# Two input projections moved between the quarters of a state-space output, and a silu rewritten by tanh

## The chip, the cores and the metric

The kernel runs on one core of one Trainium2 chip. The metric is device time in microseconds of one launch, lower is better. The core has TensorE (PE, the matmuls), VectorE (DVE), ScalarE (ACT), GpSimd (POOL) and SyncE (SP, which issues the weight DMAs). All engines read one static order of instructions each, and meet by semaphores.

## What is computed

Two layers of a decoder trunk on 272 tokens (16 meta tokens and 256), width 1024, all in float32. Each layer is a half-step feed-forward block, a mixer and another half-step feed-forward block. The change lies in the mixer alone:

```
proj = rmsnorm(h) @ w_in        # columns: sb q, k, v | deltanet qkv, z, b, a | s5 u
o_sb = rmsnorm(stick_breaking_attention(q, k, v))
o_dn = rmsnorm(gated_delta_rule(silu(conv(qkv)), b, a), dn_out_norm) * silu(z)
y    = gelu(s5_scan(u));  o_s5 = rmsnorm(y * sigmoid(y @ w_glu + b_glu))
h   += concat(o_sb, o_dn, o_s5) @ w_out
```

So z is wanted only by the last product of the DeltaNet group, and v only by the attention's outputs.

## The kernel before

Activations lie transposed, 128 channels by 272 tokens. Every product with a weight matrix is made of three matmuls in a 32-bit matmul type with a high and a low part (`mm3`, lines 144 to 146): high by high, high by low, low by high. `weights` (L134 to L139) loads 512 KB of weights, casts the high part on ACT (L136) and makes the low part by a subtraction on DVE, or on POOL for the calls of a mixer whose running number stands in `ON_POOL` (5, 7, 10, 15, 20, 25). The raw tile has 3 buffers, the high part 3, the low part 2. One **unit** is one such load and the 24 matmuls of one block of 128 output channels; `proj` (L1364) then scales it on DVE out of PSUM.

PSUM tiles go by tags (`a` to `d`) of two buffers each, and a tag's buffers are given out in the order of the program text. So a tile of a tag waits for the tile two before it in the text, whatever its priority. Here the `b` tag is used in this order: the increments of the S5 scan (`pinc`, L821, four quarters of two tiles), then the DeltaNet's `pn`, `pl`, `plt`, `pv`, `pvt` (L1088 to L1111), then the four quarters of S5's outputs (`pY`, L850 and L852). The `c` tag is used by the transposes of v (`pvs`, L1216) and after them by the attention's scores (`pz`, L1227 to L1231); `pvn`, `pS`, `pk`, `pkt` and the DeltaNet's inverse (`px` and `py`, L1016 to L1068, by `dn_inverse`) use `d`.

A scheduler orders the instructions of each engine ahead of time by its own estimate of when they are ready; `high_priority` blocks go first among those that are ready: `first()` (4000) for the DeltaNet, `second()` (1500) for S5's outputs, the GLU and its root; the rest goes by the order of the text. The steps of a mixer are written in the order of `ORD = "czsrqgbmn"`: four more convolution units, the z units with their silu, the S5 scan, the DeltaNet's rest, the six units of q, k and v, S5's outputs with the GLU, the attention, the root of S5, the DeltaNet's norm. After them `WOUT = "SnY"` gives the output projection: the S5 rows, the last products of the DeltaNet (`dn_out`), the other rows.

`s5_outputs` makes, for each of four quarters, 12 float32 matmuls into one `b` tile and four gelu activations out of it. `glu` then splits the result (L1278, L1279), multiplies it by two weight tiles (`pglu`) and takes a tanh (L107).

Of the kernel before, what the change touches and what calls it, by code (L numbers as in the profile page):

```python
# [13 lines left out]
AF = mybir.ActivationFunctionType  # L14
ALU = mybir.AluOpType
# [3 lines left out]
P = 128  # L19
NMETA = 16  # L20
SEQ = 256
T = NMETA + SEQ
# [6 lines left out]
DEPTH = 2  # L29
NQ = 16  # L30
NCH = T // 4
# [6 lines left out]

FIRST, SECOND, URGENT, THIRD = 4000, 1500, 0, 0
SBP = 0  # L40
ORD = "czsrqgbmn"
WOUT = "SnY"
OTAG, NTAG, ZT = "d", "c", "cccd"
HORD = (0, 1, 4, 2, 5, 3, 8, 6, 7, 9)
# [6 lines left out]
SET_SILU = "silu_and_others"  # L51
# [4 lines left out]
def bc(ap, axis, n):  # L56
    return ap.unsqueeze(axis).to_broadcast([*ap.shape[:axis], n, *ap.shape[axis:]])


def f32(ap):  # L60
    return ap.bitcast(F32)


class Trunk:
    def __init__(self, ctx, tc, a, out):
        self.ctx, self.tc, self.nc, self.a, self.out = ctx, tc, tc.nc, a, out
        pool = lambda n, b, **k: ctx.enter_context(tc.tile_pool(name=n, bufs=b, **k))
        self.const = pool("const", 1)
        self.res = pool("res", 1)
        self.raw = pool("raw", NBUF[2])  # L70
        self.wsp = pool("wsp", 2)
        self.small = pool("small", 1)
        self.ps = pool("ps", 1, space=PSUM)
        self.load_ins, self.set = None, None
        self.first = []
        self.since = []
        self.nw = 0
        self.on_pool = ()
        self.blocks = (0, 4)


    def psum(self, tag, nm):
# [58 lines left out]

    def mm3(self, p, wh, wl, xh, xl, first, last):
        mm = self.nc.tensor.matmul
        mm(p, wh, xh, start=first, stop=False)  # L144
        mm(p, wh, xl, start=False, stop=False)  # L145
        mm(p, wl, xh, start=False, stop=last)  # L146

# [125 lines left out]
    def load_params(self, prm):  # L273
        nc, a, c = self.nc, self.a, self.const
        q = nc.sync
        row = 0
        at = {}
        for nm, pat in (("ffn1_norm", "l (b p) -> (l b) p"), ("mix_norm", "l (b p) -> (l b) p"),
                        ("ffn2_norm", "l (b p) -> (l b) p"), ("s5_out_norm", "l (b p) -> (l b) p"),
                        ("s5_b_glu", "l (b p) -> (l b) p"), ("dn_conv_w", "l k (b p) -> (l k b) p")):  # L280
            src = a[nm].rearrange(pat, p=P)
            n = src.shape[0]
            q.dma_start(prm[row:row + n, :], src)
            at[nm] = (row, n)
# [12 lines left out]
        self.s5g = g("s5_out_norm", pat="p (l b) -> p l b", l=DEPTH)  # L297
        self.bglu = g("s5_b_glu", pat="p (l b) -> p l b", l=DEPTH)
        self.cw = g("dn_conv_w", pat="p (l k b) -> p l k b", l=DEPTH, k=4)

        for t in (self.s5g, self.bglu):
            nc.vector.tensor_scalar(t, t, 0.5, None, op0=ALU.mult)
        self.dng = g("dn_out_norm", pat="p (l b) -> p l b", l=DEPTH)
        self.sbg = g("sb_out_norm", pat="p (l b) -> p l b", l=DEPTH)

    def finish_params(self, t, sel):
# [532 lines left out]
            V.tensor_tensor(z[:, 1, :, 1:], w[:, 1, :, :-1], x[:, 0, :, :-1], op=ALU.add)  # L839
            self.S.append(z)  # L840

    def s5_outputs(self, u):

        A, PE = self.nc.scalar, self.nc.tensor
        for r in range(4):
            p = self.psum("b", "pY")
            for b in range(4):
                q = 4 * b + r
                po = p[:, b * NCH:(b + 1) * NCH]
                PE.matmul(po, self.M0[:, q, :], self.U[:, r, b, :], start=True, stop=False)  # L850
                for k in range(2):
                    PE.matmul(po, self.W2[k][:, q].rearrange("p k g c -> p (k g c)"), self.S[r][:, k, b], start=False, stop=k == 1)  # L852
            for t in range(4):
                o = u[32 * r:32 * r + 32, :, t * NCH:t * NCH + NCH]
                self.act(o, p[32 * t:32 * t + 32, :T].rearrange("p (b c) -> p b c", b=4), AF.Gelu_apprx_tanh)

# [15 lines left out]
    @staticmethod  # L872
    def hsl(h):
        return slice(64 * (h % 2), 64 * (h % 2) + 64)
# [307 lines left out]
        self.newton(r, R, t)  # L1182
        V.tensor_tensor(o, o, bc(r, 2, 64), op=ALU.mult)

    def dn_out(self, zg, slot):

        nc = self.nc
        V, G, A, PE = nc.vector, nc.gpsimd, nc.scalar, nc.tensor
        o, hsl = self.o, self.hsl
        od = self.dn_tile([P, 2, 64], "od")  # L1190
        G.tensor_copy(od, bc(o[:, 8], 1, 2))
        for b in range(2):
            po = self.psum("d", "po")
            for c in range(2):
                PE.transpose(po[:, c * P:c * P + P], o[:, 4 * c + 2 * b:4 * c + 2 * b + 2].rearrange("p h d -> p (h d)"), self.ident)
            PE.transpose(po[:, 256:256 + P], od.rearrange("p x d -> p (x d)"), self.ident)
            y = self.c288("dy")[:, :T]
            V.tensor_tensor(y[:, :256], po[:, :256], zg[:, b, :256], op=ALU.mult)
            for h in (2 * b, 2 * b + 1):
                V.tensor_tensor(y[hsl(h), 256:T], po[hsl(h), 256 + 32 * h:256 + 32 * h + 16], zg[hsl(h), b, 256:T], op=ALU.mult)  # L1200
            A.activation(self.xh[:, slot + b, :], y, AF.Copy)
            V.tensor_tensor(self.xl[:, slot + b, :], y, f32(self.xh[:, slot + b, :]), op=ALU.subtract)


    def sb(self, l, q, k, v, slot):
# [111 lines left out]
    def mixer(self, l, nxt):  # L1317
        nc, a = self.nc, self.a
        V, G, A, PE = nc.vector, nc.gpsimd, nc.scalar, nc.tensor
        w_in, w_out = a["w_in"][l], a["w_out"][l]  # L1320
        t0 = NMETA if l == DEPTH - 1 else 0
        first = lambda: self.tc.high_priority(FIRST)
        second = lambda: self.tc.high_priority(SECOND)
        self.norm_end()
        R = self.R
        self.on_pool, self.nw = ON_POOL, -1
        with ExitStack() as es:
# [26 lines left out]
            u = tmp.tile([P, 4, T], F32, name="s5u")  # L1354
            for b in range(4):
                p, = self.unit(w_in[:, 1800 + b * P:1800 + b * P + P], P, "ba"[b % 2])
                i = lambda t: t.rearrange("p (c j) -> p c j", j=4)
                V.tensor_tensor(u[:, b, :].rearrange("p (j c) -> p c j", j=4), i(p[:, :T]), i(R), op=ALU.mult)
            zr = tmp.tile([P, 2, T], F32, name="pz")

            def proj(c0, dst):
                for b in range(2):
                    p, = self.unit(w_in[:, c0 + b * P:c0 + b * P + P], P)
                    V.scalar_tensor_tensor(dst[:, b, :], p[:, :T], 0.125 if c0 == 0 else 1.0, R, op0=ALU.mult, op1=ALU.mult)  # L1364

            q, k, v = (tmp.tile([P, 2, T], F32, name=f"p{n}") for n in "qkv")

            def do_z():
                proj(1536, zr)
                self.phase(SET_SILU)  # L1370
                for b in range(2):
                    self.act(zr[:, b, :], zr[:, b, :], AF.Silu)
                    V.tensor_scalar(zr[:, b, :], zr[:, b, :], self.dng[:, l], None, op0=ALU.mult)

            def do_s5():
                with self.tc.high_priority(THIRD):
# [4 lines left out]
                    self.dn_rest(qkv)  # L1381

            def do_qkv():
                for c0, dst in ((0, q), (256, k), (512, v)):
                    proj(c0, dst)

            def do_sb():
                with self.tc.high_priority(SBP):
# [8 lines left out]
            def do_glu():  # L1397
                with second():
                    self.phase(SET_GELU)
                    self.s5_outputs(u)  # L1400
                    self.acc = self.glu(l, u)
                    self.phase(SET_LNEXP)

# [4 lines left out]
            def do_r5():  # L1408
                with second():
                    self.rms(self.acc, 4 * 512, 0, self.R5, "b")  # L1410

            steps = dict(z=do_z, s=do_s5, r=do_rest, q=do_qkv, b=do_sb, c=do_conv, g=do_glu, n=do_norm, m=do_r5)
            for x in ORD:
                steps[x]()

# [23 lines left out]
            for x in WOUT:  # L1439
                if x == "n":  # L1440
                    with first():
                        self.dn_out(zr, 2)
                    continue
                if x == WOUT[-1]:
                    self.norm_begin(*nxt)
                for d0 in (4, 6, 0, 2):
                    w_out_part(x, d0, "ab"[d0 // 2 % 2])
                    if x == WOUT[-1]:
                        for d in {4: (4, 5), 6: (6, 7), 0: (), 2: (0, 1, 2, 3)}[d0]:
                            self.norm_block(d, d0 == 2, t0)  # L1450
# [44 lines left out]
```

## Time and profile before

| | us |
|---|---|
| median of 3 runs | 1191.51 (1189.88 to 1191.59) |
| the profiled execution, its own time | 1194.31 |
| its span, first to last instruction | 1192.5 |
| TensorE busy | 1154.8 (97%) |
| VectorE busy | 853.6 (72%) |
| ScalarE busy | 614.1 (52%) |
| mean granted clock of TensorE | 0.972 |

The page of the profile cuts the span into 40 slices and gives each engine's busy share and the clock that TensorE was granted (1.00 is 2.4 GHz, 0.50 is 1.2 GHz). The two mixers lie at about 230 to 400 and 818 to 995 us, and there alone the slices show a lower clock and idle time of TensorE. Busy time of TensorE is no measure of its speed: a matmul at half the clock is busy twice as long.

### The profile page before, as it was taken

The page shows a single profiled execution, that of the slowest core. Times are in us where ns is not written, and L with a number is a line of the kernel's source. Part 1 is how long each engine was busy: PE and PEld are TensorE (multiplying, and loading weights), DVE is VectorE, ACT ScalarE, POOL GpSimd, SP SyncE. Part 2 cuts the span into 40 slices and gives each one's busy share as a digit, 9 for nine tenths or more (in the row PEclk, how much of TensorE's full clock was granted, in tenths as well). Part 3 has the DMA queues.
Part 4 walks back from the last instruction along what each step waited for, and adds up shares of the span by engine and source line. Part 5 has one row for each costly group of instructions (what it writes and reads, how often), then busy time and mean ns, then how long its engine had stood idle before and what let it go on. Part 6 is the DMA issues. An engine that isn't in the chain of part 4 may idle for free.

```text
span 1192.5 us, 23762 instructions
## 1 busy us (share of the span) xinstructions
PE 1154.8 (97%) x9544; PEld 1104.5 (93%) x9544; DVE 853.6 (72%) x1648; ACT 614.1 (52%) x981; POOL 175.3 (15%) x210
## 2 busy tenths in 40 slices
PE   8999999999998999999999999999999989999997
PEld 7999999998786999999999999999988969999985
DVE  7999986699636866555579998756994268666644
ACT  6455575564166654444455556645632566555533
POOL 6312100021010111110201112011210001111100
PEclk9999999999789999999999999999997599999999
DMA  5656545543201455555565555455431015666663
GB/s 182 179 175 180 166 135 160 167 125 108 71 19 54 142 175 177 168 176 171 177 187 177 169 173 172 132 175 156 124 112 33 27 45 185 181 188 191 187 191 117
DMA packets 196858, 173.74 MB, mean 146 GB/s; under 512 B 21300, under 2 KB 193004, under 8 KB 196748
## 3 DMA queue, kind: packets, MB, share of 16 engines
q1 hardware_dynamic: 196732, 172.22, 48.2%
q8 instruction: 75, 1.23, 0.4%
q14 instruction: 35, 0.29, 0.1%
q10 hardware_dynamic: 16, 0.00, 0.0%
HBM read 171.15 MB, written 1.05 MB: 144 GB/s over the span
## 4 chain that ended last, share of the span: by engine, by line
PE 84%; DVE 10%; ACT 3%; issue 1%; DMA 1%; SPq 0%; ACTq 0%; DVEq 0%
PE proj L146 17%; PE proj L145 17%; PE proj L144 17%; PE pd L146 5%; PE pd L145 5%; PE pd L144 5%; PE pd L493 5%; DVE wl L139 2%; PE pY L852 1%; DVE qkv L1346 1%; DVE xT L1437 1%; PE pY L850 1%; PE pl L887 1%; PE pm L783 1%; PE pz L1227 1%
## 5 line engine op out<-in xcount | busy, mean ns | idle before, releaser
L144 PE MATMUL proj<-xh,wh 128*128 128x272 f32 (+1 forms) x1840 | 521.1, 289 | 6.3 <-DVE sy L1435 2.8
L145 PE MATMUL proj<-xl,wh 128*128 128x272 f32 (+1 forms) x1840 | 518.4, 287 | 0.2 <-DVE xl L1296 0.2
L146 PE MATMUL proj<-xh,wl 128*128 128x272 f32 (+1 forms) x1840 | 492.8, 290 | 3.3 <-DVE wl L139 3.0
L136 ACT ACTIVATE wh<-raw 128x1024 fp32r<-128x1024 f32 (+1 forms) x324 | 338.2, 1044 | 292.8 <-PE proj L145 99.5
L139 DVE TENSOR_TENSOR wl<-raw,wh 128x1024 fp32r<-128x1024 f32 (+1 forms) x312 | 378.4, 1213 | 146.6 <-PE pd L146 60.9
L144 PEld LDWEIGHTS proj<-xh,wh 128*128 128x128 f32 x1840 | 345.4, 188 | 10.5 <-DVE sy L1435 4.1
L145 PEld LDWEIGHTS proj<-xl,wh 128*128 128x128 f32 x1840 | 345.2, 188 | 3.0 <-issue 1.5
L146 PEld LDWEIGHTS proj<-xh,wl 128*128 128x128 f32 x1840 | 328.8, 187 | 7.2 <-DVE wl L139 5.8
L144 PE MATMUL pd<-hh,wh 128*128 128x272 f32 x528 | 149.6, 288 | 0.0
L145 PE MATMUL pd<-hl,wh 128*128 128x272 f32 x528 | 149.3, 288 | 0.0
L435 POOL TENSOR_TENSOR hl<-h,hh 128x272 fp32r<-128x272 f32 (+1 forms) x88 | 81.1, 924 | 452.9 <-ACT hh L434 452.8
L146 PE MATMUL pd<-hh,wl 128*128 128x272 f32 x528 | 140.8, 288 | 0.2
L144 PEld LDWEIGHTS pd<-hh,wh 128*128 128x128 f32 x528 | 99.2, 188 | 0.2
L145 PEld LDWEIGHTS pd<-hl,wh 128*128 128x128 f32 x528 | 99.3, 188 | 0.1
L146 PEld LDWEIGHTS pd<-hh,wl 128*128 128x128 f32 x528 | 95.1, 188 | 1.0 <-DVE wl L139 0.9
L107 ACT ACTIVATE g<-g 128x272 f32<-128x272 f32 (+2 forms) x92 | 37.6, 415 | 68.9 <-DVE g L429 68.8
L433 DVE TENSOR_TENSOR h<-proj,g 128x272 f32<-128x272 f32 (+1 forms) x88 | 37.7, 433 | 32.9 <-PE proj L146 21.3
L434 ACT ACTIVATE hh<-h 128x272 fp32r<-128x272 f32 (+1 forms) x88 | 36.4, 419 | 47.1 <-DVE h L433 47.1
L429 DVE TENSOR_TENSOR g<-proj,R 128x272 f32<-128x272 f32 (+1 forms) x88 | 37.5, 430 | 17.8 <-PE proj L146 17.6
L139 POOL TENSOR_TENSOR wl<-raw,wh 128x1024 fp32r<-128x1024 f32 x12 | 30.7, 2557 | 110.5 <-ACT th L107 34.9
L431 DVE TENSOR_TENSOR g<-g,R 128x272 f32<-128x272 f32 (+1 forms) x88 | 37.7, 432 | 12.6 <-ACT g L107 12.3
L376 POOL TENSOR_TENSOR acc<-acc,sq 128x272 f32<-128x272 f32 (+1 forms) x20 | 22.7, 1134 | 91.4 <-ACT sq L370 90.5
(490 smaller groups left out, 1310.1 us busy)
## 6 DMA issues: line engine op xcount, KB each, us to landing
raw<-in_ffn_w_gate_dram SPq DMA_DIRECT2D x88, 512.0 KB, 3.6
raw<-in_ffn_w_up_dram SPq DMA_DIRECT2D x88, 512.0 KB, 3.6
raw<-in_ffn_w_down_dram SPq DMA_DIRECT2D x70, 512.0 KB, 3.5
raw<-in_w_in_dram SPq DMA_DIRECT2D x36, 512.0 KB, 4.4
raw<-in_ffn_w_down_dram SPq DMA_DIRECT2D x24, 384.0 KB, 3.0
raw<-in_w_out_dram SPq DMA_DIRECT2D x16, 512.0 KB, 3.5
raw<-in_s_w_glu_dram SPq DMA_DIRECT2D x4, 512.0 KB, 3.4
xin<-in_x_dram SPq DMA_DIRECT2D x4, 256.0 KB, 5.8
```

The lines of the kernel that those rows point to most:

```text
L107: i = self.nc.scalar.activation(out, in_, func, **k)
L136: nc.scalar.activation(h[:, :n], r[:, :n], AF.Copy)
L139: e.tensor_tensor(l[:, :n], r[:, :n], f32(h[:, :n]), op=ALU.subtract)
L144: mm(p, wh, xh, start=first, stop=False)
L145: mm(p, wh, xl, start=False, stop=False)
L146: mm(p, wl, xh, start=False, stop=last)
L429: V.tensor_tensor(g1, pg[j][:, :N], R, op=ALU.mult)
L431: V.tensor_tensor(g1, g1, R, op=ALU.mult)
L433: V.tensor_tensor(h, pu[j][:, :N], g1, op=ALU.mult)
L434: nc.scalar.activation(hh[:, f, :N], h, AF.Copy)
L435: G.tensor_tensor(hl[:, f, :N], h, f32(hh[:, f, :N]), op=ALU.subtract)
L493: PE.matmul(pd[i][e], x[:, f, ts], w[:, 0, e * 512:e * 512 + 512], start=f == 0 and w is h and x is hh, stop=f == NF - 1 and w is lo)
```

## The change

The z units leave their place behind the convolutions and the v units theirs behind k. `s5_outputs` now makes one quarter at a time, and after each quarter comes one unit: v's two blocks, then z's two. An ordering edge (no semaphore, both are on TensorE) puts the first matmul of each unit behind the last matmul of its quarter. The units, their weight loads and casts are now written inside the `second()` block, and ahead of the GLU's. Since the running number of the weight calls shifts, the call numbered 10 (on POOL) is q's first block in place of z's first, and number 15 is v's second in place of k's second.

z's silu is no longer one Silu activation and a multiplication by the norm's gain: it is a tanh of z/2 (ACT), then (tanh + 1) z in one DVE operation. The factor one half goes into the gain `dng`, which is halved once at the start; the gain itself is applied in `dn_out` as the scale of the two operations that split the product.

```diff
-ORD = "czsrqgbmn"
+ORD = "csrqgbmn"
     def mm3(self, p, wh, wl, xh, xl, first, last):
-        mm(p, wh, xh, start=first, stop=False)
+        i = mm(p, wh, xh, start=first, stop=False)
+        if self.behind is not None:
+            self.order(getattr(i, "ins", i), self.behind)
+            self.behind = None
-        for t in (self.s5g, self.bglu):
+        for t in (self.s5g, self.bglu, self.dng):
             nc.vector.tensor_scalar(t, t, 0.5, None, op0=ALU.mult)
     def dn_out(self, zg, g, slot):
-            A.activation(self.xh[:, slot + b, :], y, AF.Copy)
-            V.tensor_tensor(self.xl[:, slot + b, :], y, f32(self.xh[:, slot + b, :]), op=ALU.subtract)
+            A.activation(self.xh[:, slot + b, :], y, AF.Copy, scale=g)
+            V.scalar_tensor_tensor(self.xl[:, slot + b, :], y, g, f32(self.xh[:, slot + b, :]), op0=ALU.mult, op1=ALU.subtract)
-            def do_z():
-                proj(1536, zr)
-                self.phase(SET_SILU)
-                for b in range(2):
-                    self.act(zr[:, b, :], zr[:, b, :], AF.Silu)
-                    V.tensor_scalar(zr[:, b, :], zr[:, b, :], self.dng[:, l], None, op0=ALU.mult)
+            def do_z(b):
+                proj(1536, zr, b)
+                t = self.cv("zt")[:, :T]
+                self.act(t, zr[:, b, :], AF.Tanh, scale=0.5)
+                V.scalar_tensor_tensor(zr[:, b, :], t, 1.0, zr[:, b, :], op0=ALU.add, op1=ALU.mult)
             def do_qkv():
-                for c0, dst in ((0, q), (256, k), (512, v)):
+                for c0, dst in ((0, q), (256, k)):
             def do_glu():
                 with second():
                     self.phase(SET_GELU)
-                    self.s5_outputs(u)
+                    units = (proj, 512, v, 0), (proj, 512, v, 1), (do_z, 0), (do_z, 1)
+                    for r, (f, *args) in enumerate(units):
+                        self.behind = self.s5_outputs(u, r)
+                        f(*args)
                     self.acc = self.glu(l, u)
```

`s5_outputs(u, r)` is the body of the old loop over r, and returns its last matmul; `proj(c0, dst, b)` is the body of the old loop over b.

## Rows read from the trace of the kernel before

**Rows 1.** The page: busy us and share of the engines; the granted clock by slice.
```profile
PE 1154.8 (97%) x9544; PEld 1104.5 (93%) x9544; DVE 853.6 (72%) x1648; ACT 614.1 (52%) x981; POOL 175.3 (15%) x210
...
PEclk9999999999789999999999999999997599999999
```
**Rows 2.** Busy us by stretch, first mixer: window, length, PE PEld DVE ACT POOL, clock, DMA.
```profile
264.00:308.00 44.00, 39.89 (x315) 37.42 (x313) 43.68 (x90) 16.82 (x26) 7.86 (x7) 1.00 0.41 120
308.00:325.00 17.00, 16.86 (x292) 13.99 (x292) 9.17 (x20) 1.17 (x5) 0.11 (x1) 0.51 0.10 33
325.00:343.10 18.10, 17.30 (x303) 16.56 (x296) 3.33 (x8) 8.91 (x24) 3.18 (x5) 0.96 0.01 3
343.10:357.80 14.70, 13.74 (x95) 13.10 (x95) 7.60 (x13) 9.46 (x19) 2.61 (x1) 0.82 0.13 37
357.80:384.80 27.00, 23.92 (x175) 17.87 (x175) 16.45 (x43) 17.43 (x37) 0.44 (x1) 1.00 0.19 59
```
**Rows 3.** The same view of three of the four mixer stretches at half the clock.
```profile
341.69:348.52 6.83, 5.99 (x31) 5.80 (x30) 1.92 (x5) 2.88 (x9) 0.74 (x1) 0.50 0.00 0
898.08:911.72 13.64, 13.64 (x294) 10.83 (x297) 6.85 (x16) 1.07 (x3) 0.11 (x1) 0.50 0.02 4
...
925.38:949.27 23.89, 23.46 (x119) 22.29 (x118) 4.88 (x15) 9.71 (x23) 2.35 (x1) 0.50 0.07 23
```
**Rows 4.** VectorE by line, 264 to 309 us: shapes, count, busy us, mean ns.
```profile
L139 DVE TENSOR_TENSOR wl<-raw,wh 128x1024 fp32r<-128x1024 f32 x8 | 9.7, 1211 | 0.0
```
**Rows 5.** Engines in time: start, us, engine, line, operation, shapes, [idle before it <- by].
```profile
276.29 0.42 DVE L1364 SCALAR_TENSOR_TENSOR pz<-proj,R 128x272 f32<-128x272 f32 x1
276.64 1.20 DVE L139 TENSOR_TENSOR wl<-raw,wh 128x1024 fp32r<-128x1024 f32 x1
277.77 0.74 DVE L989 TENSOR_TENSOR r<-LT,id 128x576 f32<-128x576 f32 x1
...
279.56 0.34 DVE L1373 TENSOR_SCALAR pz<-pz,prm 128x272 f32<-128x272 f32 x1
```
**Rows 6.** The same for GpSimd and VectorE, about 287 us.
```profile
286.55 3.10 POOL L139 TENSOR_TENSOR wl<-raw,wh 128x1024 fp32r<-128x1024 f32 x1 [1.42 <-PE proj L146]
...
288.08 1.64 DVE L1006 TENSOR_TENSOR TT<-TT,t 128x54 f32<-128x54 f32 x1
```
**Rows 7.** The same for TensorE, 304 to 309 us and about 325 us.
```profile
307.36 0.54 PE L1216 MATMUL pvs<-ident,pv 128*128 128x128 f32 x2 [2.11 <-DVE pv L1364]
308.14 0.99 PE L1088 MATMUL pn<-bd,sq 128*128 128x2 f32 x4 [0.25 <-DVE x L826]
...
324.76 0.32 PE L1111 MATMUL pvt<-ident,qkv 64*32 64x64 f32 x8
325.00 0.44 PE L850 MATMUL pY<-s5U,M 128*128 128x68 f32 x2
```
**Rows 8.** By stretch, the attention's tiles alone: pz, then pvs (PE first).
```profile
304.70:325.00 20.30, 4.58 (x18) 2.58 (x12) 0.00 (x0) 0.00 (x0) 0.58 0.17 54
...
304.70:325.00 20.30, 1.57 (x6) 0.51 (x6) 1.01 (x3) 0.58 0.17 54
```
**Rows 9.** By stretch, inside a feed-forward block: PE, PEld, DVE, ACT, POOL.
```profile
460.00:470.00 10.00, 10.00 (x82) 10.00 (x81) 6.09 (x9) 5.50 (x8) 1.67 (x2) 1.00 0.53 161
```
**Rows 10.** By stretch, the inverse's tiles alone: px, then py.
```profile
325.00:343.10 18.10, 2.85 (x64) 2.59 (x64) 0.86 (x2) 1.09 (x3) 0.96 0.01 3
...
325.00:343.10 18.10, 3.29 (x136) 2.87 (x136) 1.71 (x4) 0.37 (x1) 0.96 0.01 3
```
**Rows 11.** TensorE in time: the GLU's first matmul.
```profile
343.14 0.82 PE L144 MATMUL pglu<-xh,wh 128*128 128x272 f32 x2 [0.84 <-ACT xh L1278]
```
**Rows 12.** By stretch, DeltaNet tiles after the GLU: pvn, then pS.
```profile
357.80:384.80 27.00, 1.08 (x8) 0.97 (x8) 0.36 (x1) 1.00 0.19 59
...
357.80:384.80 27.00, 1.49 (x16) 1.28 (x16) 1.54 (x5) 0.00 (x0) 1.00 0.19 59
```
**Rows 13.** ScalarE in time, about 358 us.
```profile
357.82 1.28 ACT L97 ACT_TABLE_LOAD   x1
```

More of the change, by code (lines that the diff above doesn't have):

```diff
@@ L143, in mm3 @@
         mm = self.nc.tensor.matmul
-        mm(p, wh, xh, start=first, stop=False)
+        i = mm(p, wh, xh, start=first, stop=False)
+        if self.behind is not None:
+            self.order(getattr(i, "ins", i), self.behind)
+            self.behind = None
         mm(p, wh, xl, start=False, stop=False)
@@ L299, in load_params @@
         self.cw = g("dn_conv_w", pat="p (l k b) -> p l k b", l=DEPTH, k=4)
-        for t in (self.s5g, self.bglu):
+        self.dng = g("dn_out_norm", pat="p (l b) -> p l b", l=DEPTH)
+        for t in (self.s5g, self.bglu, self.dng):
             nc.vector.tensor_scalar(t, t, 0.5, None, op0=ALU.mult)
-        self.dng = g("dn_out_norm", pat="p (l b) -> p l b", l=DEPTH)
         self.sbg = g("sb_out_norm", pat="p (l b) -> p l b", l=DEPTH)
@@ L840, in s5, with s5_outputs @@
             self.S.append(z)
[L842 to L855, printed above, removed]
+    def s5_outputs(self, u, r):
+        PE = self.nc.tensor
+        p = self.psum("b", "pY")
+        for b in range(4):
+            q = 4 * b + r
+            po = p[:, b * NCH:(b + 1) * NCH]
+            PE.matmul(po, self.M0[:, q, :], self.U[:, r, b, :], start=True, stop=False)
+            for k in range(2):
+                i = PE.matmul(po, self.W2[k][:, q].rearrange("p k g c -> p (k g c)"), self.S[r][:, k, b], start=False, stop=k == 1)
+        for t in range(4):
+            o = u[32 * r:32 * r + 32, :, t * NCH:t * NCH + NCH]
+            self.act(o, p[32 * t:32 * t + 32, :T].rearrange("p (b c) -> p b c", b=4), AF.Gelu_apprx_tanh)
+        return getattr(i, "ins", i)
     def dn_tile(self, sh, nm, b=1):
@@ L1183, in dn_norm, with dn_out @@
         V.tensor_tensor(o, o, bc(r, 2, 64), op=ALU.mult)
-    def dn_out(self, zg, slot):
+    def dn_out(self, zg, g, slot):
         nc = self.nc
@@ L1359, in mixer, with proj @@
             zr = tmp.tile([P, 2, T], F32, name="pz")
-            def proj(c0, dst):
-                for b in range(2):
-                    p, = self.unit(w_in[:, c0 + b * P:c0 + b * P + P], P)
-                    V.scalar_tensor_tensor(dst[:, b, :], p[:, :T], 0.125 if c0 == 0 else 1.0, R, op0=ALU.mult, op1=ALU.mult)
+            def proj(c0, dst, b):
+                p, = self.unit(w_in[:, c0 + b * P:c0 + b * P + P], P)
+                V.scalar_tensor_tensor(dst[:, b, :], p[:, :T], 0.125 if c0 == 0 else 1.0, R, op0=ALU.mult, op1=ALU.mult)
             q, k, v = (tmp.tile([P, 2, T], F32, name=f"p{n}") for n in "qkv")
-            def do_z():
-                proj(1536, zr)
-                self.phase(SET_SILU)
-                for b in range(2):
-                    self.act(zr[:, b, :], zr[:, b, :], AF.Silu)
-                    V.tensor_scalar(zr[:, b, :], zr[:, b, :], self.dng[:, l], None, op0=ALU.mult)
+            def do_z(b):
[3 more added lines that the diff above has]
+                V.scalar_tensor_tensor(zr[:, b, :], t, 1.0, zr[:, b, :], op0=ALU.add, op1=ALU.mult)
             def do_s5():
@@ L1383, in do_qkv @@
             def do_qkv():
-                for c0, dst in ((0, q), (256, k), (512, v)):
-                    proj(c0, dst)
+                for c0, dst in ((0, q), (256, k)):
+                    for b in range(2):
+                        proj(c0, dst, b)
             def do_sb():
@@ L1410, in do_r5 @@
                     self.rms(self.acc, 4 * 512, 0, self.R5, "b")
-            steps = dict(z=do_z, s=do_s5, r=do_rest, q=do_qkv, b=do_sb, c=do_conv, g=do_glu, n=do_norm, m=do_r5)
+            steps = dict(s=do_s5, r=do_rest, q=do_qkv, b=do_sb, c=do_conv, g=do_glu, n=do_norm, m=do_r5)
             for x in ORD:
@@ L1441, in mixer @@
                     with first():
-                        self.dn_out(zr, 2)
+                        self.dn_out(zr, self.dng[:, l], 2)
                     continue
```

## The prediction, made before the changed kernel was run

> **What bounds the kernel now.** I read the page first: TensorE is busy for 97% of the span, and its granted clock leaves full speed only in two places, the mixers [rows 1]. A busy TensorE says little there, so I read each mixer by stretches. In the first mixer they are: A, 264 to 308 us, where projections run beside the S5 scan; B, to 325, the DeltaNet's products through the `b` tiles; C, to 343.1, S5's outputs and the DeltaNet's inverse; D, the GLU; E, the attention's chain up to 384.8 [rows 2]. In A VectorE is busy for 43.68 of 44 us and TensorE has 4.1 us idle, most of it in one wait of 2.11 us for v's scaling on VectorE [rows 2, 7]: A ends when VectorE's list is done. In B TensorE is busy for 16.86 of 17 us, at a clock of 0.51, that is nearly all of it at 1.2 GHz; VectorE is half idle [rows 2]. In C TensorE bounds at nearly the full clock, and ahead of D it waits 0.84 us for the split of the last gelu [rows 2, 11]. In E it is idle for 3.1 of 27 us; there the attention's steps through ScalarE and PSUM set the length. The second mixer has the same order of work, but its clock is worse: it falls at 925.38 us, in the middle of its C, and comes back after 23.89 us, at the end of its D, where the first mixer lost 6.83 us [rows 3].
>
> So four units, 96 matmuls, leave a stretch that VectorE bounds and enter one that TensorE bounds. By that alone the change loses. It can gain in what VectorE sheds in A, in what leaves B, and in the clock of C and D.
>
> **A, less VectorE work.** In A lie eight casts of low parts on VectorE [rows 4] (by the running numbers: z's second block, both of q, k's first, both of v, and already both of the GLU's) and two on GpSimd (z's first, k's second). Since each of the two low buffers waits for the unit two before it, after the change the casts of z and of the GLU can't come before v's matmuls, which now lie in C. Left on VectorE are q's second, k's two and v's first: four fewer, at 1.13 us from start to start (276.64 to 277.77) [rows 5], 4.5 us. Four scalings go, 0.35 us each (276.29 to 276.64), 1.4 us, and two products with z's gain, 0.34 us each less some overlap, 0.5 us [rows 5]. The GpSimd casts cost VectorE too: beside one, an operation on 54 columns took 1.64 us [rows 6]; but there are two before and two after, so this term stands. Sum 6.4 us. In the emptier A the scan's matmuls may meet half the clock, which could give back a little; I take -6, ends -5 and -6.4. TensorE will be idle in A for some 6 us more (four units less, 11.7 us by the price below, in a stretch 6 us shorter), which costs nothing while VectorE bounds.
>
> **B, fewer matmuls at half the clock.** v comes later, and the scores wait for v's transposes, since both are given the `c` tiles in the order of the text. So `pz` (4.58 us) and the last third of `pvs` (about 0.6 of 1.57 us) leave B [rows 8]: 5.2 us of TensorE time in a stretch that TensorE filled. If B is then bound by the chain through the two `b` buffers instead (`pn` starts 0.25 us after a VectorE release, and `pY` directly after `pvt` [rows 7]), nothing is gained. I take -5, ends 0 and -5.2, because TensorE, not VectorE, was full.
>
> **The inverse.** `px` and `py` take 2.85 and 3.29 us in C [rows 10]. Their input is a chain of small VectorE steps in A, which was threaded between casts. With a lighter VectorE list and idle TensorE time at the end of A and in B, they can move ahead of C: between 0 and -6.1 us; I take the middle, -3.
>
> **C, the units.** At full clock 82 matmuls take 10 us [rows 9], so a unit of 24 takes 2.93 us and four take +11.7 us. Their scalings, casts, tanh and (tanh + 1) z fall on VectorE and ScalarE, which are busy for 3.3 and 8.9 of 18.1 us in C [rows 2]: nothing, under TensorE's cover. z's last unit covers the gelu and its split, so the wait of 0.84 us goes (0.4 in the second mixer, from a busy time of 23.46 in 23.89 us [rows 3]). The weight DMAs keep their order and number on SyncE. The new edge is between two instructions of TensorE's own queue; behind a held unit stand the next quarter and the DeltaNet's products, but its operands are ready long before. The table load before the attention [rows 13] stays one, since tanh already follows gelu there without another.
>
> **The clock in C and D.** At half the clock matmul time doubles, so low stretches of 6.83 and 23.89 us [rows 3] cost at most 3.4 and 11.9 us. What the rows show is that the clock fell although TensorE was busy: it was busy for 13.64 of 13.64 us in 898.08 to 911.72 [rows 3], with scores, small products and the inverse. It came back in the D of both mixers, where the GLU's matmuls ran. The units are matmuls of the same form, so C should hold 2.4 GHz better. I take half in the first mixer, -1.7 (0 to -3.4), and -8.5 in the second (0 to -11.9), assuming that it keeps one low stretch as short as the first's.
>
> The Trainium skill ("TensorE: Matmul & The Clock Gate", section "HAM oscillation — how this bites in real kernels") speaks against this term: it lays the fall of the clock to gaps in which TensorE idles. Taken so, the change digs such gaps into A and fills a C that had none, and the clock terms would be zero or worse; the trace bears that out only for A's end, not for 925 us. What it would give is the second rival.
>
> **What comes back later.** v's transposes and the scores must still run: about 6 us at half the clock in B and the end of A [rows 8], some 4 at full. E's idle 3.1 us [rows 2] can take about half; I take +2 (0 to +4). The DeltaNet's steps get ahead of the GLU and lengthen the way to its end, while E, bound by the attention's chain, hardly shrinks: `pvn` 1.08 and `pS` 1.49 us [rows 12], and two smaller ones of about half a us each; +1.8 (0 to +3.6).
>
> The rest is small: the splits in `dn_out` carry a scale, +0.1 us on each of four blocks, and the halving of the gain is one short VectorE operation under the first feed-forward block: +0.5 in all.
>
> **The sum.** First mixer: -6 -5 -3 +11.7 -0.8 -1.7 +2 +1.8 = -1.0. Second: -6 -5 -3 +11.7 -0.4 -8.5 +2 +1.8 = -7.4. With +0.5: **-7.9 us**. The profiled execution took 1194.3 us, 1.8 of it outside its span; it would take 1186.4. The median of the runs is 2.8 us lower, so on it I predict 1191.5 - 7.9 = **1183.6 us**.
>
> **The rivals.**
>
> First, slower: the `b` chain sets B. If releases and not TensorE pace `pn` to `pvt`, B keeps its length and the inverse stays in C: 8 us less gain in each mixer, -7.9 + 16 = +8.1, 1199.6 us. It decides for slower once B and the inverse together give under half of the 8 us. For it: each product there is followed by a VectorE step before its buffer is free. Against: TensorE was full in B, VectorE half idle. Chance 0.18.
>
> Second, the clock doesn't answer: low stretches stay as long, in C or moved to E. Then -1.7 and -8.5 fall out: +2.3 us, 1193.8, no change or a little slower. For it: A will be emptier, so the clock may fall earlier. Against: the units are what brought it back in D. Chance 0.17.
>
> Third, more: the inverse fits ahead of C whole (-6.2 more) and no low stretch is left after B (-5.1 more): -19.2, 1172.3. For it: much idle TensorE time at the end of A. Against: small tiles that end inside C would pull the clock down once more. Chance 0.14.
>
> Fourth, the change doesn't do what it says: the edge only says what a unit comes after, not that it comes at once. If the scheduler puts the units in a lump behind the last quarter, the clock is gained only from there on, about half of that term: -2.8, 1188.7. Chance 0.06.
>
> **How the numbers follow.** The forecast has 0.45. A measurement of this kernel can tell about 0.2%, 2.4 us. Faster: nearly all of the forecast (0.43), the third (0.14), most of the fourth (0.04): 0.61. Within: the rest of the forecast and the fourth (0.04), two thirds of the second (0.11), a little of the first (0.01): 0.16. Slower: 0.23. The range reaches from the third rival to just short of the first: 1172 to 1197.
>
> **What would show it.** Right: VectorE's full stretch ends about 6 us earlier; `pY` starts 10 to 12 us earlier, its quarters with a unit behind each; `px` and `py` begin before B; the full clock holds from C to E in the second mixer. The forecast fails if `pY` starts less than 8 us earlier, or if the second mixer still shows over 15 us at half the clock after its B. TensorE idle in A for over 15 us would be right and harmless, unless the clock falls there so early that q and k come late.

## The result and the profile after

The changed kernel takes 1197.47 us (median of 4 runs, 1196.18 to 1198.20), against 1190.70 us (1187.84 to 1191.59) for the kernel before beside it: a ratio of 1.006 (95% 1.0039 to 1.0081), 6.8 us slower. The forecast was 1183.6 us, and its range ended at 1197. In single executions of two kernels below one mixer stayed at half the clock for 47.8 and 58.0 us; the ratios and their intervals leave out executions over 1.5% above the fastest of their kernel, the medians leave out none.

The page after, busy us of each engine and the granted clock by slice:

```profile
PE 1146.0 (96%) x9544; PEld 1097.9 (92%) x9544; DVE 856.8 (72%) x1649; ACT 614.5 (51%) x981; POOL 174.2 (15%) x210
...
PEclk9999999998799999999999999999978989999999
```

TensorE is busy for 8.8 us less than in [rows 1] and the clock dips no deeper, and yet the kernel is slower. So the mixers have to be read by stretches once more. The first mixer after, with the columns of [rows 2]: A and B together, then A from 262.6 us, then B, C (from the first `pY` to the first `pglu`), the GLU's matmuls, and E from there to the last matmul of `dn_out` (`po`; the prediction lets the GLU's stretch D end 3.5 us later, at 357.8 us, and E begin there):

```profile
231.50:312.80 81.30, 71.67 (x726) 66.42 (x724) 74.56 (x156) 35.82 (x61) 12.40 (x13) 0.86 0.33 92
262.60:300.70 38.10, 28.47 (x216) 26.65 (x214) 37.70 (x79) 11.71 (x18) 7.11 (x7) 0.85 0.34 97
300.70:312.80 12.10, 12.10 (x273) 10.83 (x273) 9.10 (x21) 0.58 (x2) 0.11 (x1) 0.50 0.01 3
...
312.80:347.50 34.70, 34.70 (x448) 33.56 (x445) 11.35 (x24) 15.21 (x35) 3.19 (x5) 1.00 0.16 47
347.50:359.20 11.70, 11.70 (x109) 9.98 (x109) 6.72 (x16) 6.13 (x14) 2.37 (x1) 1.00 0.27 87
359.20:387.00 27.80, 22.82 (x142) 16.15 (x142) 15.61 (x33) 20.20 (x40) 0.29 (x1) 1.00 0.18 59
```

In A VectorE is still busy for 37.70 of 38.10 us, and four casts of low parts remain on it where [rows 4] has eight:

```profile
L141 DVE TENSOR_TENSOR wl<-raw,wh 128x1024 fp32r<-128x1024 f32 x4 | 4.9, 1214 | 0.0
```

B went from 17 us [rows 2] to 12.1. C went from 18.1 us to 34.7, all of them filled by TensorE at full clock: 16.6 us more, where four units cost 11.7. And the stretch of the GLU holds 109 matmuls, where the same one of the kernel before has 73:

```profile
343.10:354.30 11.20, 11.16 (x73) 10.80 (x73) 4.33 (x8) 5.96 (x14) 2.61 (x1) 0.76 0.06 12
```

The long stretches at half the clock now lie at the end of A and in B (first two lines), and C and the GLU have the full clock in both mixers (last two):

```profile
289.23:313.12 23.89, 16.12 (x290) 14.72 (x290) 20.75 (x53) 0.80 (x2) 0.34 (x3) 0.50 0.07 24
883.15:903.63 20.48, 14.08 (x208) 13.13 (x208) 18.20 (x47) 0.40 (x1) 0.34 (x3) 0.50 0.07 24
...
903.60:958.20 54.60, 52.24 (x671) 48.10 (x669) 23.57 (x50) 28.88 (x60) 3.75 (x5) 1.00 0.18 59
313.10:388.00 74.90, 68.92 (x686) 59.39 (x685) 34.47 (x75) 41.42 (x87) 5.84 (x7) 1.00 0.19 57
```

TensorE's timeline after (start, us, line, operation, idle time before it in brackets), of the end of A, the seam from B to C and the start of the GLU:

```profile
300.66 0.99 PE L1093 MATMUL pn<-bd,sq 128*128 128x2 f32 x4 [2.39 <-DVE x L831]
...
304.93 0.31 PE L1021 MATMUL px<-T,Lm 32*32 32x32 f32 x5
...
312.42 0.44 PE L1116 MATMUL pvt<-ident,qkv 64*32 64x64 f32 x8
312.79 0.58 PE L854 MATMUL pY<-s5U,M 128*128 128x68 f32 x2
...
347.52 0.37 PE L146 MATMUL pglu<-xh,wh 128*128 128x272 f32 x1
...
349.35 0.38 PE L1221 MATMUL pvs<-ident,pv 128*16 128x128 f32 x2
349.66 0.72 PE L1232 MATMUL pz<-pq,pk 64*128 64x272 f32 x2
...
355.00 0.27 PE L1164 MATMUL pkt<-qkv,kn 64*32 64x64 f32 x3
```

The last lines are the find: v's last transposes, the first scores and the DeltaNet's `pkt` run between the GLU's matmuls. What ran from the first `pY` to the GLU's end, one tile to a line (PE busy us come first; `pvn`, `pS`, `pkt`, `pz`, `pvs`, `px`, `py` in this order):

```profile
312.80:359.20 46.40, 2.11 (x16) 2.04 (x16) 0.75 (x2) 1.00 0.19 57
312.80:359.20 46.40, 2.97 (x32) 2.56 (x32) 1.54 (x5) 0.54 (x2) 1.00 0.19 57
312.80:359.20 46.40, 0.84 (x16) 0.52 (x16) 0.47 (x2) 1.00 0.19 57
312.80:359.20 46.40, 2.67 (x18) 1.55 (x12) 1.75 (x4) 0.86 (x2) 1.00 0.19 57
312.80:359.20 46.40, 0.98 (x6) 0.65 (x6) 1.01 (x3) 1.00 0.19 57
312.80:359.20 46.40, 2.85 (x64) 2.59 (x64) 0.86 (x2) 0.94 (x3) 1.00 0.19 57
312.80:359.20 46.40, 3.06 (x136) 2.70 (x136) 1.71 (x4) 0.75 (x2) 1.00 0.19 57
```

In the first mixer of the kernel before, `pvn` and `pS` alone of the first five came between the first `pY` and the GLU's end (325 to 354.3 us), both with half as many matmuls:

```profile
325.00:354.30 29.30, 1.90 (x8) 1.97 (x8) 0.37 (x1) 0.88 0.03 6
325.00:354.30 29.30, 1.49 (x16) 1.28 (x16) 0.00 (x0) 0.54 (x2) 0.88 0.03 6
```

Where the time went, in us from the first matmul of the root of the norm ahead of a mixer (`pms`, the same instruction in all traces; at 232.9 and 821.0 us in the kernel before, 231.5 and 824.0 after). "The root" below is this one; `hh` is the feed-forward block's. "before again" is a second profiled execution of the kernel before (below); the other rows are the experiments of the next section.

| mixer 1 / mixer 2 | first `pY` | GLU's first matmul | GLU's end | end of the last `po` | next block's first `hh` activation |
|---|---|---|---|---|---|
| before | 92.1 / 91.3 | 110.2 / 112.4 | 121.4 / 128.9 | 151.7 / 156.7 | 188.9 / 192.4 |
| before again | 91.0 / 91.3 | 109.1 / 112.7 | 120.0 / 124.4 | 150.3 / 153.3 | 187.5 / 189.0 |
| after | 81.3 / 80.7 | 116.0 / 114.2 | 127.7 / 126.9 | 155.2 / 154.9 | 193.4 / 191.9 |
| z alone behind quarters 3, 4 | 84.2 / 84.3 | 109.7 / 109.8 | 118.6 / 118.7 | 146.7 / 146.5 | 184.2 / 184.4 |
| after, DeltaNet tail late | 80.9 / 81.0 | 111.4 / 111.5 | 121.9 / 121.9 | 151.6 / 151.5 | 187.9 / 187.1 |
| after, transposes in `b` | 81.3 / 81.1 | 116.2 / 114.5 | 125.4 / 125.0 | 154.1 / 152.9 | 192.5 / 190.2 |
| after, both | 80.9 / 79.9 | 111.4 / 110.3 | 121.1 / 120.0 | 149.3 / 148.3 | 187.0 / 184.2 |

### The profile page after: what moved, and what is told of

Same layout as the page of the kernel before. It is cut to its first block, busy times and chain, and to the rows that moved or that the text cites. A ratio compares the mean times of both kernels' runs of the same rounds, so it can differ in the third digit from the quotient of the medians.

```text
span 1195.1 us, 23770 instructions
## 1 busy us (share of the span) xinstructions
PE 1146.0 (96%) x9544; PEld 1097.9 (92%) x9544; DVE 856.8 (72%) x1649; ACT 614.5 (51%) x981; POOL 174.2 (15%) x210
## 3 DMA queue, kind: packets, MB, share of 16 engines
q1 hardware_dynamic: 196732, 172.22, 47.8%
## 4 chain that ended last, share of the span: by engine, by line
PE 86%; DVE 9%; ACT 2%; issue 1%; DMA 1%; POOL 0%; SPq 0%; ACTq 0%; DVEq 0%; POOLq 0%
PE proj L151 18%; PE proj L150 17%; PE proj L146 17%; PE pd L151 5%; PE pd L150 5%; PE pd L146 5%; PE pd L498 5%; DVE wl L141 2%; PE pY L856 1%; PE pl L892 1%; DVE s5z L837 1%; PE pm L788 1%; DVE qkv L1351 1%; PE pY L854 1%; PE pz L1247 1%
## 5 line engine op out<-in xcount | busy, mean ns | idle before, releaser
L138 ACT ACTIVATE wh<-raw 128x1024 fp32r<-128x1024 f32 (+1 forms) x324 | 338.1, 1044 | 278.2 <-PE proj L150 80.7
L150 PE MATMUL pd<-hl,wh 128*128 128x272 f32 x528 | 149.3, 288 | 0.0
```

The costliest lines, as they stand in the source:

```text
L138: nc.scalar.activation(h[:, :n], r[:, :n], AF.Copy)
```

## The experiments

**How far one trace carries: before again, and the tanh alone.** The first is the kernel before without an edit. The second is the kernel before with z's silu rewritten as in the change and the units left where they were:

```diff
-                    self.act(zr[:, b, :], zr[:, b, :], AF.Silu)
-                    V.tensor_scalar(zr[:, b, :], zr[:, b, :], self.dng[:, l], None, op0=ALU.mult)
+                    t = self.cv("zt")[:, :T]
+                    self.act(t, zr[:, b, :], AF.Tanh, scale=0.5)
+                    V.scalar_tensor_tensor(zr[:, b, :], t, 1.0, zr[:, b, :], op0=ALU.add, op1=ALU.mult)
```

> The kernel before, unchanged. The trace of before held 23.9 us at half the clock behind S5's outputs of the second mixer, and 8.5 us of the forecast's gain stood on taking that away. If that stretch belongs to the kernel, this second trace shows it again (over 15 us at half the clock after 920 us), its own time is near the 1194.3 us of the first trace, and the forecast failed in the terms of C. If it was a chance of that one execution, the second mixer here shows some 7 us after its B, like the first mixer, the execution takes about 1190 us, and 8 us of the forecast's gain were never there. Ratio to before 1.000 in both.

> Only the rewriting of z's silu (tanh, gain halved and carried by the two splits in dn_out); the units stay in their old places. If the loss comes from where the units lie, this is the same as before within 2 us: two products of 0.27 us leave VectorE and two of 0.35 us come, and the splits cost 0.1 us more on four blocks. If the rewriting is what costs, it shows most of the 6.8 us here, 1196 to 1198 us.

Measured: 1189.89 us, 1.0005 (0.9975 to 1.0034), and 1189.90 us, 0.9997 (0.9968 to 1.0027). The rewriting costs nothing that can be measured, within some 3 us. But the stretches at half the clock differ from [rows 3] in each profiled execution. In the second mixer of "before again", behind its B:

```profile
923.94:937.59 13.65, 13.22 (x72) 12.42 (x71) 1.91 (x5) 4.92 (x14) 0.00 (x0) 0.50 0.00 0
...
947.83:951.24 3.41, 3.32 (x22) 2.91 (x21) 0.78 (x2) 3.40 (x7) 0.00 (x0) 0.50 0.48 153
```

and of the tanh alone:

```profile
930.31:937.13 6.82, 6.24 (x35) 6.05 (x34) 1.91 (x5) 2.97 (x9) 0.00 (x0) 0.50 0.00 0
```

So the 23.89 us of the second mixer, from which the forecast took its largest term, belonged to one execution; in the two others that stretch was 17.06 and 6.82 us. That execution lay 3.6 us above the median of the kernel before (1194.31 against 1190.70).

**z alone, and v alone.** z's units behind quarters 3 and 4 with v's in their old place; v's behind quarters 1 and 2 with z's in theirs:

```diff
-                for c0, dst in ((0, q), (256, k)):
+                for c0, dst in ((0, q), (256, k), (512, v)):
...
-                    units = (proj, 512, v, 0), (proj, 512, v, 1), (do_z, 0), (do_z, 1)
+                    units = None, None, (do_z, 0), (do_z, 1)
```

```diff
-ORD = "csrqgbmn"
+ORD = "czsrqgbmn"
...
-                    units = (proj, 512, v, 0), (proj, 512, v, 1), (do_z, 0), (do_z, 1)
+                    units = (proj, 512, v, 0), (proj, 512, v, 1), None, None
```

> The change with v left behind k in its old place; z's two units behind the third and fourth quarter. If what counts is TensorE work put ahead of the GLU's end, the two units add 5.9 us there, VectorE sheds about 3.5 us in A, v's transposes and the scores stay in B, and the wait of 0.84 us goes: about 1 us per mixer, 1190 to 1194 us in all, and the second loss of the change (v's transposes and scores behind the units) is absent. If the emptier A with its earlier fall of the clock is what costs, half of the emptying gives half of the loss, 1193 to 1195 us, and the clock falls some 8 us earlier than in before, not 18.

> The change with z left in its old place (by tanh); v's two units behind the first and second quarter. If TensorE work ahead of the GLU's end counts: A ends about 4 us earlier, B is 5 us shorter without transposes and scores, 5.9 us of units and up to 5 us of transposes and scores come back before the GLU's end, and the DeltaNet's steps with them: 1 to 3 us slower per mixer, 1193 to 1197 us, so more of the loss than z alone. If the emptier A costs, it is about the same as z alone.

> Once more z's units behind quarters 3 and 4 with v in its old place, for a second trace and more times. If TensorE work ahead of the GLU's end sets the time, both mixers show what the second mixer of the first trace showed: v's transposes end about 69 us after the root, pY starts at 85, the GLU ends at 120 and the last po at 148, against 78, 91, 121 to 129 and 150 to 157 before and 118, 81, 127 and 155 in the change. If the earlier start of pY is what counts, the change, which has the earliest, would be ahead of it.

Measured: z alone 1182.02 us, 0.9902 (0.9865 to 0.9939), and again 1182.87 us, 0.9940 (0.9922 to 0.9959); v alone 1190.76 us, 0.9982 (0.9962 to 1.0003). Neither was expected: z alone was put at 1190 to 1195 us, v alone at 1193 to 1197. So z's half of the change is worth about 8 us, v's half alone nothing that can be measured, and v's half on top of z's costs 14.6 us (1197.47 less 1182.87). The trace of z alone (of the second run, an execution of 1180.04 us) tells why it gains; TensorE's timeline, then C, the GLU and E of the first mixer:

```profile
295.44 0.44 PE L1221 MATMUL pvs<-ident,pv 128*128 128x128 f32 x2 [1.09 <-DVE pv L1368]
...
299.99 1.27 PE L1232 MATMUL pz<-pq,pk 64*128 64x272 f32 x2
```

```profile
315.90:341.40 25.50, 25.50 (x375) 24.58 (x369) 7.03 (x15) 12.81 (x31) 3.19 (x5) 1.00 0.07 22
341.40:350.30 8.90, 8.90 (x76) 8.53 (x75) 5.07 (x12) 4.60 (x11) 2.48 (x1) 1.00 0.22 64
350.30:378.60 28.30, 24.04 (x175) 17.74 (x174) 19.15 (x43) 21.43 (x42) 0.29 (x1) 1.00 0.23 74
```

With z out of A, v comes 8 us earlier: its transposes start 63.8 us after the root (71.9 before) and the scores 68.3 us after it (78.0 before). The 18 matmuls of the first scores then all run ahead of the `pn` with which B begins, where TensorE had idle time (4.3 us from the root to the last `pn` before, 2.6 now), and B loses them without v having moved: the last `pn` starts 2.5 us earlier, and from there to `pY` it takes 9.4 us in place of 14.7. `pY` starts 84.2 us after the root in place of 92.1. C and the GLU hold, beside their own work and two units, 5.5 us of the DeltaNet's `pvn`, `pS` and `pk`, but none of the scores, the transposes and `pkt`.

**What stood in the way after: the DeltaNet's tail and the tile order.** In the changed kernel the DeltaNet's steps behind `pvt` (`pk`, `pvn`, `pS`, `pkt`) go ahead of the GLU, as they are in a block of the highest priority; in the first experiment they have the ordinary one:

```diff
# dn_rest, behind vbt
+        yield
# do_rest
+                g = self.dn_rest(qkv)
                 with first():
-                    self.dn_rest(qkv)
+                    next(g)
+                next(g, None)
```

> The change, with the DeltaNet's steps behind its pvt (pvn, pS, pk, pkt, pvt2) at the ordinary priority, not ahead of S5's outputs and the GLU. They took about 8 us of TensorE between pY's start and the GLU's end in the change, and their result is wanted only 20 us after the last of them. If the attention's stretch E starts with the GLU's end and is bound by its own chain, the GLU's end comes 5 to 8 us earlier per mixer and the time falls by 4 to 14 us, 1183 to 1193. If TensorE work as such is the bound to the end of the mixer, the steps only change places: within 2 us of the change's 1197.

Measured: 1186.72 us, 0.9970 (0.9958 to 0.9983), 10.8 us less than the changed kernel (which was not run again; the kernel before took 1190.70 us beside it, 1190.82 beside this one and 1190.81 beside the next two). C, the GLU and E of its first mixer:

```profile
313.10:343.60 30.50, 30.50 (x411) 29.71 (x405) 9.77 (x19) 14.48 (x32) 3.19 (x5) 1.00 0.17 54
343.60:354.10 10.50, 10.50 (x89) 9.50 (x87) 5.23 (x11) 7.01 (x16) 2.45 (x1) 1.00 0.30 100
354.10:384.00 29.90, 26.68 (x197) 20.28 (x197) 19.00 (x45) 20.43 (x41) 0.44 (x1) 1.00 0.17 54
```

The edit does not move all of it: 3.9 of the 7.5 us of these steps still come ahead of the GLU's end, but of the scores only 1.3 us in place of 2.7. C is now 30.5 us, the 18.1 of before and the 11.7 of four units with 0.7 beside them. The GLU ends 5.8 and 5.0 us earlier. `pkt` runs 12.5 us later in the first mixer, and that costs less than the GLU gains: `po` ends 3.6 and 3.4 us earlier, the next block starts 5.5 and 4.8 earlier.

The second experiment gives v's transposes `b` tiles, so that the scores no longer stand behind them in the `c` tiles; the third has both edits:

```diff
-            pv = psum("pvs")
+            pv = self.psum("b", "pvs")
```

> The change with v's transposes in the b buffers, so that the first scores no longer stand behind them in the c buffers and can run as soon as q and k are there. If the scores' return ahead of the GLU's end is part of the loss, they now start about 68 us after the mixer's root, in TensorE's idle end of A, instead of 118; the GLU's end comes 3 to 4 us earlier per mixer, and the time falls by 4 to 8 us, 1189 to 1193. If only the units count, or if the scores lengthen B at half the clock by as much as they free in the GLU, the time stays within 2 us of 1197.

> The same with the DeltaNet's steps behind pvt at the ordinary priority. If both the scores and these steps cost by standing ahead of the GLU's end, the gains add: 1180 to 1184 us against 1186.7 with the steps late alone. If the room behind the GLU's end is by then taken, 1185 to 1189.

Measured: 1194.41 us, 1.0034 (1.0018 to 1.0051), between the two cases expected, and 1183.49 us, 0.9941 (0.9920 to 0.9962), as expected if the gains add. The scores now start in A; TensorE's timeline of the second experiment:

```profile
286.68 0.72 PE L1232 MATMUL pz<-pq,pk 64*128 64x272 f32 x2
```

That is 55 us after the root, where the changed kernel has them at 118. C, the GLU and E of the third:

```profile
313.80:344.30 30.50, 30.50 (x409) 29.72 (x405) 9.78 (x19) 14.49 (x32) 3.19 (x5) 1.00 0.18 54
344.30:354.00 9.70, 9.70 (x88) 9.17 (x85) 5.59 (x14) 6.91 (x16) 2.46 (x1) 1.00 0.28 87
354.00:382.40 28.40, 24.26 (x182) 18.23 (x180) 17.80 (x41) 20.72 (x41) 0.29 (x1) 1.00 0.20 64
```

The two edits give 10.8 and 3.1 us alone and 14.0 together: the gains add, and together they are all of the change's 6.8 us and 7.2 more. The 3.1 us alone are the weaker number, since the intervals of that kernel and of the change overlap; the table has the GLU's end 2.3 and 1.9 us earlier. And the costs are not wholly apart, since the first edit also put half of the scores behind the GLU's end. The four units do fit into C with a gain, once nothing else comes along with them. This kernel and z alone beat both the kernel before and the changed one; its 7 times lie between 1182.81 and 1187.69.

**Other places for z.** Behind quarters 1 and 2, and behind 1 and 4, with v in its old place:

```diff
-                    units = None, None, (do_z, 0), (do_z, 1)
+                    units = (do_z, 0), (do_z, 1), None, None
```

```diff
+                    units = (do_z, 0), None, None, (do_z, 1)
```

> v stays in its old place, z's two units behind the first and second quarter, not the third and fourth. If TensorE work ahead of the GLU's end sets the time, the place within C hardly matters: the GLU's end comes as in the run with quarters 3 and 4 (120 us after the mixer's root, 127 in the change), but for 1 to 2 us of gelu that is no longer covered: 1181 to 1185 us. If the gain of that run came from covering the wait for the last gelu, it is gone here, over 1187 us. The profile of that run kept half the clock for 58 us in its first mixer; with units directly behind the first quarter no low stretch should last beyond the second quarter.

> v stays in its old place, z's units behind the first and the last quarter: one early in C, one that covers the last gelu. By the theory that TensorE work ahead of the GLU's end sets the time: 1179 to 1183 us, the lower side of the runs with z alone, and no low stretch beyond the second quarter. By the rival that the place within C matters little for the clock: the same spread as behind quarters 3 and 4.

Measured: 1187.55 us, 0.9972 (0.9946 to 0.9997), and 1193.76 us, 1.0032 (1.0019 to 1.0045). The first lies just where it was put for the case that the cover of the last gelu was what gained; the second misses both of its cases. Behind 1 and 2 the GLU starts about 3.9 us after the last `pY`, since no unit covers the last gelu, and half the clock is back there, for 6.8 us in the first mixer and 3.4 in the second. Behind 1 and 4 half the clock came back inside C of both mixers; the first line is the stretch ahead of the first fall:

```profile
325.00:333.48 8.48, 8.48 (x128) 8.22 (x127) 2.23 (x5) 3.30 (x9) 0.00 (x0) 1.00 0.20 64
333.48:343.71 10.23, 10.23 (x56) 9.99 (x54) 0.86 (x2) 3.19 (x9) 1.80 (x1) 0.50 0.01 2
...
927.39:937.62 10.23, 10.23 (x56) 9.99 (x55) 0.42 (x1) 3.31 (x10) 0.00 (x0) 0.50 0.00 0
```

TensorE is busy in every microsecond of these, and was so for 8 us and more ahead of both falls, so idle time is not what took the clock there. What did is open. With the changed kernel's units, or with z's behind 3 and 4, C kept it in the traces shown here; but in another execution of z alone, of 1202.53 us, half the clock lasted from the end of A through C of the first mixer, those 58.0 us.

**What z and v cost at all.** The kernel before without z's units, and z behind quarters 3 and 4 without v's:

```diff
-                proj(1536, zr)
+                self.nw += 2
+                for b in range(2):
+                    A.copy(zr[:, b, :], R)
```

```diff
-                for c0, dst in ((0, q), (256, k), (512, v)):
+                for c0, dst in ((0, q), (256, k)):
+                self.nw += 2
...
-                    self.sb(l, q, k, v, 0)
+                    self.sb(l, q, k, k, 0)
```

> The kernel before without z's two units (a copy stands in for z, so the gate is wrong; the running numbers of the casts are kept). It prices these units where they lay. If TensorE work in A is covered by VectorE, as the forecast had it, they cost only their VectorE share there, about 3.5 us per mixer: 1183 to 1185 us. If they cost more than that because they also hold up v, whose transposes and scores then miss the idle end of A and fall into B, leaving them out gives 6 to 8 us per mixer: 1175 to 1179 us, with v's transposes 8 us earlier and pY 6 to 7 us earlier, as with z behind quarters 3 and 4. The difference of that run (1182) to this one is then what the units cost in C: 2 to 4 us per mixer, not 5.9.

> z behind quarters 3 and 4, and v's two units left out (the attention reads k in place of v, so its output is wrong; running numbers kept). It prices v's units: against z behind 3 and 4 (1182) where they lay, in A, and against the change (1197) behind quarters 1 and 2. If A, once z is gone from it, covers v's units and the transposes and scores behind them, v costs 1 to 3 us per mixer there: 1176 to 1180 us, so the change pays 8 to 10 us per mixer for v in C (5.9 of units, the rest transposes and scores ahead of the GLU's end). If TensorE's work counts the same everywhere, v in A costs 5 to 6 us per mixer: 1170 to 1172 us.

Measured: 1175.52 us, 0.9890 (0.9856 to 0.9925), and 1187.46 us, 0.9974 (0.9939 to 1.0009). The times of the first lie between 1172.71 and 1186.56, so what follows is rough. By the ratio z's units cost 13 us where they stood, 1.1% of 1190.5, though A has idle TensorE time, and their move to C takes back about half of it (0.9940 against 0.9890). They were not free in A, since v waited behind them: in the trace without them the last `pn` starts 3.7 and 3.4 us earlier, VectorE's share as it was expected, and from there to `pY` another 4.4 and 6.1 us go, with v's transposes 7.4 and 8.7 us earlier. The second result misses what was expected by 7 us and more. Leaving out v brought the GLU's end 2 us earlier than in z alone, and then E took 34.5 us in place of 28.1, with a stretch at half the clock that z alone does not have, in both mixers:

```profile
352.45:366.10 13.65, 13.57 (x75) 10.99 (x76) 7.94 (x20) 10.14 (x19) 0.00 (x0) 0.50 0.23 72
...
939.54:953.19 13.65, 13.65 (x76) 11.03 (x77) 8.20 (x21) 10.03 (x19) 0.00 (x0) 0.50 0.25 78
```

In the 4 us ahead of each fall TensorE had been idle for about 1.4. So v's price in A stays open.

**Both gains at once?** z alone with the DeltaNet's tail late, by the edit shown above:

> The two things that gained, together: z behind quarters 3 and 4 with v in its old place, and the DeltaNet's steps behind pvt at the ordinary priority. If both act by the GLU's end, on which the attention's stretch hangs, the steps (pvn, pS, pk; about 5 us of TensorE before the GLU's end in that run) go behind it: 1174 to 1180 us against 1182. If the attention's stretch is by then full of TensorE work, they lengthen it by as much: 1180 to 1185.

Measured: 1192.57 us, 1.0005 (0.9977 to 1.0032), a miss. The traced execution took 1186.97 us, 5.6 us under that median. In it `pY` starts 87.2 us after the root in both mixers, 3 us later than in z alone, with the scores 3.3 us later (71.6), and E takes 29.6 and 31.2 us. The edit made C 1.3 us shorter (24.2 against 25.5), but why the way to `pY` grew was not found.

## Why the prediction was wrong

By the table, the sum of each mixer against the same execution before, mixer 1 / mixer 2, with the forecast's 0.5 us of small terms left out:

| stretch | forecast | measured | against "before again" |
|---|---|---|---|
| root to first `pY` (A, B) | -11 / -11 | -10.8 / -10.6 | -9.7 / -10.6 |
| first `pY` to the GLU's end (inverse, units, wait, clock, DeltaNet) | +8.0 / +1.6 | +17.1 / +8.6 | +17.4 / +13.1 |
| GLU's end to last `po` (E) | +2 / +2 | -2.8 / +0.2 | -2.8 / -0.9 |
| from there to the next block | 0 / 0 | +1.0 / +1.3 | +1.0 / +1.3 |
| sum | -1.0 / -7.4 | +4.5 / -0.5 | +5.9 / +2.9 |

**Right: A and B.** The last `pn` starts 6.1 and 5.2 us earlier (forecast 6), with VectorE full and four casts fewer, as told, and B gave the other 4.7 and 5.4 (forecast 5). The first rival, that the chain of the `b` tiles would hold B's length, did not happen: B's 12.1 us are full of TensorE. The rival's sign came true by another mechanism. TensorE's idle time before 300.7 us grew as told, to 9.6 of 38.1 us, and the clock did fall earlier there, at 289 us, without undoing the 11 us.

**Wrong: the inverse (-3).** `px` and `py` still take 5.9 us in C, where they took 6.1 [rows 10]. The bound of zero was the true value. The idle time lay at the end of A, but `px` starts at 304.93 us, in a B that TensorE fills.

**Right: the units, the wait and that the clock of C would hold.** Full clock from 313.1 to 388 us, and for 54.6 us behind the second mixer's B; the wait of 0.84 us [rows 11] is gone.

**Wrong: what else enters C.** This is the step "What comes back later". The forecast put v's transposes and the scores into the idle time of E, and gave the DeltaNet's steps 1.8 us. In the trace the 17.1 us of the first mixer are: units 11.7; DeltaNet's steps 7.5 against 3.5 before, +4.0 (`pvn` 2.11, `pS` 2.97, `pkt` 0.84 and `pk` 1.6, where before `pvn` with 1.90, `pS` with 1.49 and 0.1 of `pk` came ahead of the GLU's end); scores and transposes 2.67 and 0.98, +3.7; the wait -0.8; about -1.5 is what is left, put down to the clock and not shown apart. And E did not give it back: it shrank by 2.8 us in one mixer and not at all in the other. The experiments show the size: the DeltaNet's tail late is worth 10.8 us, the scores ahead of v's transposes 3.1, both 14.0, where the forecast had (1.8 + 2) for each mixer, 7.6, for both together. Both causes were at hand: the text says that the DeltaNet's steps get ahead of the GLU, and that the scores wait for v's transposes. What was missing is by how much. `pkt` starts 123.5 us after the root in the changed kernel and 124.3 in z alone, at the same time; but in z alone the GLU has ended by then (118.6), while four units push it to 127.7, behind the tail.

**Wrong: the size of the clock term (-8.5).** It was worked out from a stretch of 23.89 us that two other executions show as 17.06 and 6.82. Worked out as there (half of what is above 6.83 us), "before again" would have given 5.1 us, and the execution with the tanh nothing. The same fault lies in the last line of the sum: the gain was taken off the median, and the execution that it was read from lay above the median by 3.6 us. The rule that the forecast weighed, of the Trainium skill ("TensorE: Matmul & The Clock Gate", section "HAM oscillation — how this bites in real kernels"), lays the fall of the clock to gaps in which TensorE idles. The changed kernel's A and B agree, with TensorE busy for 16.12 of 23.89 us at half the clock; the 10.23 of 10.23 us with z behind quarters 1 and 4, and the 8.48 of 8.48 us ahead of the first of these stretches, do not.

**Missed: that half of the change is better than the whole.** Nothing in the forecast asked what each group of units was worth alone. z alone gains 8 us, because in A its units held up v and with v the transposes and scores that filled B. Had v stayed, "v comes later" would have been "v comes earlier", and B would have been emptied all the same.

Of the two signs put down for a failure, `pY` starting less than 8 us earlier and over 15 us at half the clock behind the second mixer's B, neither came: both watched the terms that held.

Open is why the clock falls in C or E of some of these kernels and not of others, why the tail's move gains 10.8 us in one and loses 10 in another, and where the 1.0 to 1.3 us behind the mixers come from.

## What to carry to other kernels

When work is moved out of a stretch, ask of each tile that waits behind it, by priority and by the order in which buffers are given out, where it will run next: a stretch made longer takes in whatever of higher priority comes ready before its end. Try the halves of a change alone, since one of them may carry the gain and the other undo it. A term that rests on a clock stretch needs more than one execution behind it, and the sum is to be set against the execution from which its terms were read.

## What was not expected of the hardware

The kernel before, run three times with a profile (one of them with the tanh, which changed no time), spent 23.89, 17.06 and 6.82 us at half the clock behind the second mixer's B, with the same order of work. And the clock can fall while TensorE is busy: with z behind quarters 1 and 4 it was busy throughout ahead of the fall and for the 10.23 of 10.23 us behind it. In the kernel before it was busy for all of the 13.64 us at full clock that end where the 23.89 us begin:

```profile
911.73:925.37 13.64, 13.64 (x261) 13.22 (x252) 3.04 (x8) 5.60 (x15) 1.38 (x4) 1.00 0.01 2
```

Less work can go with more time: without v the kernel is 4.6 us slower than with it (1187.46 against 1182.87, with intervals that overlap), with 13.65 us at half the clock in E that the traced execution of the other does not have. There idle time did come ahead of the fall.
